# Left rows of the output projections on 128 rows, value products with a pair of heads as weights, and high weights of two branches by ScalarE in a float32 decoder trunk

## The chip, the cores and the metric

One core of one Trainium2 chip runs the whole program. The time is device microseconds of one execution; less is better. The engines are TensorE (PE, with its weight loads, PEld), VectorE (DVE), ScalarE (ACT), GpSimd (POOL) and SyncE (SP), which issues the weight transfers. Each engine works through its instructions in order; waits between engines are semaphores.

## What is computed

Two layers of a decoder trunk on 256 tokens of width 1024, all in float32. A layer is a gated feed-forward block, a mixer, a cross-attention to 256 memory tokens, and a second feed-forward block. The change lies in the mixer:

```python
proj = h @ w_in
o_fox = fox_attention(fq, fk, fv, log_f).reshape(b, s, FOX_W)                           # 6 heads of 64
o_dsa = dsa_sparse_attention(dq, dk, dv, q_idx, k_idx, w_idx, topk).reshape(b, s, DSA_W)  # 5 heads
o_sb = stick_breaking_attention(sq, sk, sv).reshape(b, s, SB_W)                          # 5 heads
g = jax.nn.sigmoid(gates.reshape(b, s, N_BRANCH, D_MODEL))
merged = g[:, :, 0] * (o_fox @ w_fox_out) + g[:, :, 1] * (o_dsa @ w_dsa_out) + g[:, :, 2] * (o_sb @ w_sb_out)
return merged @ w_out
```

So the output projections contract over 384, 320 and 320 rows: three chunks of 128 rows for the first branch, two chunks of 128 and 64 left rows for the other two. In all three an attention probability matrix P of 256x256 is multiplied with the head's values, out = P V, which is the value product.

## The kernel before

**Float32 by parts.** A matrix product runs on operands that are split in a high part (rounded to the fp32r format) and a low part (the rest): high x high, high x low and low x high are added up in one accumulator (`mm3`, lines 139 to 141). The activations are split once (`split`, lines 153 and 154: ACT writes the high part, DVE the low part). The weights come by SP into `wraw` (three buffers) and are split as they come, in `load_w`: the high part `wh` by ACT (`high`, line 92) or by DVE (line 90), as `share["high"]` says, and the low part `wl` by DVE or POOL (`sub_split`, line 86). `wh` and `wl` have five buffers each.

**The left rows.** Where a weight has 64 left rows (320 = 2 x 128 + 64), `load_w` makes one block of 128 rows out of them (lines 128 to 133): rows 0 to 63 of `wl` hold the high part (a copy by ACT, line 131), rows 64 to 127 the low part. The activation's high part stands twice, in rows 0 to 63 and in rows 64 to 127 (`osplit`, line 482). Then two products do for three (`mm2`): line 145 on 128 rows gives high x high and low x high together, line 146 on 64 rows gives high weight x low activation.

**The mixer.** `softmax_pv` takes one head's logits to probabilities, transposes them on PE (line 592) and calls `pv`: two matmuls with the head's 64 columns of values as weights and the probabilities as the moving operand (lines 599 and 600). The first head of a pair writes rows 0 to 63 of a PSUM bank `ops`, the second rows 64 to 127. There is one such bank. The stick-breaking branch computes the probabilities of two heads at once and calls `pv` for both, one behind the other. The last head of branches two and three stands alone in its bank. `osplit` then splits the bank in high and low, `osp`.

**The output projections** come after the heads (lines 771 to 787). All twelve gates pass the sigmoid in a row on ACT, between two loads of its function tables. Each branch has two weight loads of 512 columns, and each load two column blocks of 256, which take one of three accumulator banks `acc`. A block is six groups of products (two halves by three chunks). DVE multiplies the block with its gate (line 783), which frees the bank; POOL adds it to the branch before (line 785). While these weights are loaded, `share["high"]` is "DVE", so DVE casts all high parts (line 90) and ACT makes only the copies of left rows. Behind this stage comes the keys' projection of the cross-attention, then the mixer's last projection.

**The order** of each engine's instructions is set by a scheduler when the program is built; the code of these parts names no order. So the change also moves instructions that it does not touch.

Of the kernel before, what the change touches and what calls it, by code (L numbers as in the profile page):

```python
# [9 lines left out]
F32 = mybir.dt.float32  # L10
# [22 lines left out]
def trunk(ctx: ExitStack, tc: tile.TileContext, x, mem, positions, ffn1_norm, ffn1_w_gu, ffn1_w_down,  # L33
# [20 lines left out]
    def o_ps():  # L54
        return psum.tile([128, 512], F32, name="ops", bufs=1)
# [41 lines left out]
    def load_w(cols, first=None):  # L97
# [6 lines left out]
        for g in first or groups(-(-rows // 128), 2048 // n):  # L104
# [14 lines left out]
            for gg in groups(g, 1024 // n):  # L119
                h = wts.tile([128, 1024], F32R, name="wh", bufs=5)  # L120
                lo = lows.tile([128, 1024], F32R, name="wl", bufs=5)
                b = min(k1 + gg, full)
                if b > k1:
                    r, o = raw[:, k1 * n:b * n], slice(0, (b - k1) * n)
                    high(h[:, o], r)
                    sub_split(lo[:, o], r, h[:, o])
                    res += [(h[:, j * n:(j + 1) * n], lo[:, j * n:(j + 1) * n]) for j in range(b - k1)]
                if k1 + gg > full:
                    r, o = raw[:, full * n:(full + 1) * n], slice((full - k1) * n, (full - k1 + 1) * n)
                    high(h[:, o], r)  # L130
                    ACT.activation(lo[:64, o], r[:64], AF.Copy)
                    sub_split(lo[64:, o], r[64:], h[64:, o])
                    res.append((h[:64, o], lo[:, o]))
                k1 += gg
# [8 lines left out]
    def mm2(ps, a, b, first, last):  # L143

        PE.matmul(ps, a[1], b[0], start=first, stop=False)
        PE.matmul(ps, a[0], b[1], start=False, stop=last)  # L146

# [312 lines left out]
    def mixer_cross(l):  # L460
# [4 lines left out]
        with tc.tile_pool(name="mix", bufs=1) as mp:  # L465
# [10 lines left out]

            def osplit(ps, n):
                h = mp.tile([128, S], F32R, name="osp", bufs=18)
                lo = mp.tile([128, S], F32R, name="osp", bufs=18)
                split(h[:n], lo[:n], ps[:n])  # L480
                if n < 128:
                    ACT.activation(h[64:], ps[:64], AF.Copy)
                return (h, lo[:n])

# [92 lines left out]

            def softmax_pv(lg, v, h, ot, b):

# [14 lines left out]
                ACT.activation(pT, ps[:, :384], AF.Copy)  # L594
                pv(ot, b, v, h, pT[:, 0:256], pT[:, 256:384])

            def pv(ot, b, v, h, p0, p1):
                o = ot[b:b + 64, :]
                PE.matmul(o, v[0][:, h * 64:(h + 1) * 64], p0, start=True, stop=False)  # L599
                PE.matmul(o[:, 128:256], v[1][:, h * 64:(h + 1) * 64], p1, start=False, stop=True)  # L600

            def tok_v(pss, n):
                res = []
                for t in range(2):
                    v = mp.tile([128, 384], F32, name="vtok", bufs=4)
                    ACT.activation(v[:, :n], pss[t][:, :n], AF.Copy, scale=rc[t])
                    res.append(v)
                return res
# [37 lines left out]
            for j in range(NFOX // 2):  # L646
# [4 lines left out]
                for c, n in ((0, 128), (256, 256)):  # L651
                    for i, ps in enumerate(bank):
                        b = slice(64 * i, 64 * i + 64)
                        PE.matmul(ps[:, c:c + n], fqk[j][b, c // 2:c // 2 + 128], fqk[3 + j][b, 0:n],  # L654
                                  start=False, stop=c == 256)
                ot = o_ps()[:, :256]
                for i, ps in enumerate(bank):
# [5 lines left out]
                                             op0=OP.add, op1=OP.add)  # L663
                    softmax_pv(lg, fv, h, ot, 64 * i)
                ofox.append(osplit(ot, 128))

# [11 lines left out]
            for j in range(3):  # L678
                nh = 2 if j < 2 else 1
                bank = scores(dT[0][j], dT[1][j], nh)  # L680
                ot = o_ps()[:, :256]
                for i, ps in enumerate(bank):
                    lg = w384()
                    DVE.tensor_tensor(lg, ps[:, :384], dmask, op=OP.add)
                    softmax_pv(lg, dv, 2 * j + i, ot, 64 * i)
                odsa.append(osplit(ot, 64 * nh))

# [28 lines left out]
            for j in range(3):  # L716
# [30 lines left out]
                tact(az, zm, AF.Exp)  # L747
                ot = o_ps()[:, :256]
                for i in range(nh):
                    pv(ot, 64 * i, sv, 2 * j + i, az[:, i, 0:256], az[:, i, 256:384])  # L750
                osb.append(osplit(ot, 64 * nh))


# [17 lines left out]
            merged = []  # L771
            share["high"], share["pool"] = "DVE", 0
            for br, (wo, ot) in enumerate(((w_fox_out, ofox), (w_dsa_out, odsa), (w_sb_out, osb))):
                for cc in range(2):
                    w = load_w([wo[l][:, cc * 512:(cc + 1) * 512]])
                    for c in (2 * cc, 2 * cc + 1):
                        ps = acc_ps()
                        for s in range(2):
                            for k in range(3):
                                mm = mm2 if br and k == 2 else mm3  # L780
                                mm(ps[:, s * 256:(s + 1) * 256], cols(w[k], 2 * (c % 2) + s), ot[k], k == 0, k == 2)
                        g = gates[br * 4 + c]
# [92 lines left out]
            for kt in range(2):  # L875
                for h in range(NCA):
                    PE.matmul(ots[h], vm[kt][:, h * 128:(h + 1) * 128], pT[h][:, kt], start=kt == 0, stop=kt == 1)
            oc = [osplit(ot, 128) for ot in ots]
            for c in range(4):
# [43 lines left out]
```

## Time and profile before

| what | before |
|---|---|
| median of 3 runs | 1345.66 us (1345.48 to 1345.84) |
| the profiled execution | 1345.4 us, its span 1343.7 us |
| PE busy | 1328.5 us, 99% of the span, 10746 matmuls |
| DVE, ACT, POOL busy | 905.8 (67%), 719.0 (54%), 292.8 us (22%) |
| granted clock of PE, mean | 0.998 |
| the chain that ended last | PE 94%, DVE 3% |
| DMA | 234.65 MB, mean 175 GB/s |

The span is the time from the first to the last instruction in the trace. The busy time of PE is counted with modelled ends, and matmuls overlap, so the cost of a product is read from the distance of starts. The chain is the work followed back from the last instruction, at each step to what released it. A float32 matmul that is not split in parts (lines 592, 599, 600 and 877) shows as two passes in the timeline, so one value product of a head counts as two rows of each of its two lines.

### The profile page before, as it was taken

Reading aid. Unit: us, or ns where it says so; the run is one execution under the profiler, and the core shown is the slowest. Engines: PE = TensorE matmul, PEld = TensorE weight load, DVE = VectorE, ACT = ScalarE, POOL = GpSimd, SP = SyncE. Lnnn points to the kernel's source line nnn. Section 1 sums busy time; section 2 is a strip of 40 time slices with the busy share of each in tenths; the row PEclk is TensorE's granted clock in tenths of the full one; section 3 lists DMA queues with packets and bytes.
Section 4 is the critical chain, followed back from the end, with each engine's and each line's share of the span. In section 5 each row is a group of like instructions: output and inputs, shape, how many; then the busy total and the mean of one; then the engine's idle time right before and its main releaser. Section 6 shows DMA issues by size and latency. Waiting matters only on the chain.

```text
span 1343.7 us, 26241 instructions
## 1 busy us (share of the span) xinstructions
PE 1328.5 (99%) x10746; PEld 1275.6 (95%) x10746; DVE 905.8 (67%) x1397; ACT 719.0 (54%) x1149; POOL 292.8 (22%) x257
## 2 busy tenths in 40 slices
PE   8999999999999999999999999999999999999998
PEld 7999998989999999999999999999989899999987
DVE  7866556965689776665666665668567886766643
ACT  6555544545754565554465554444556556655543
POOL 3211114421313122111121110334223320311100
PEclk9999999999999999999999999999999999999999
DMA  7665654645446455566655566646453554566551
GB/s 252 192 198 192 208 167 146 186 118 160 133 127 210 153 177 174 190 197 202 198 188 189 188 205 193 186 124 207 118 158 119 165 190 165 166 198 200 198 183 67
DMA packets 220712, 234.65 MB, mean 175 GB/s; under 512 B 8656, under 2 KB 209968, under 8 KB 220592
## 3 DMA queue, kind: packets, MB, share of 16 engines
q1 hardware_dynamic: 219904, 231.87, 54.3%
q8 instruction: 84, 1.38, 0.4%
q0 software_dynamic: 240, 0.55, 0.1%
q10 hardware_dynamic: 448, 0.57, 0.1%
q14 instruction: 36, 0.29, 0.1%
HBM read 231.91 MB, written 1.05 MB: 173 GB/s over the span
## 4 chain that ended last, share of the span: by engine, by line
PE 94%; DVE 3%; DMA 1%; POOL 1%; issue 1%; ACT 0%; SPq 0%; DVEq 0%; ACTq 0%; POOLq 0%
PE acc L139 29%; PE acc L141 28%; PE acc L140 28%; PE ops L599 1%; PE qk L543 1%; DMA wraw<-in_ffn_w_gu_dram 1%; PE acc L146 1%; DVE wl L86 1%; PE tr L592 1%; PE qk L728 1%; PE qk L654 1%; PE ops L600 0%; DVE sc L573 0%; POOL it L517 0%; PE qk L825 0%
## 5 line engine op out<-in xcount | busy, mean ns | idle before, releaser
L86 DVE TENSOR_TENSOR wl<-wraw,wh 128x1024 fp32r<-128x1024 f32 (+6 forms) x429 | 510.9, 1194 | 225.4 <-ACT wh L92 218.5
L92 ACT ACTIVATE wh<-wraw 128x1024 fp32r<-128x1024 f32 (+4 forms) x447 | 446.0, 1003 | 274.1 <-PE acc L140 177.1
L141 PE MATMUL acc<-xh,wl 128*128 128x256 f32 x2032 | 564.5, 278 | 1.6 <-DVE wl L86 1.6
L140 PE MATMUL acc<-xl,wh 128*128 128x256 f32 x2032 | 564.4, 278 | 0.0
L139 PE MATMUL acc<-xh,wh 128*128 128x256 f32 x2032 | 563.9, 279 | 0.0
L141 PEld LDWEIGHTS acc<-xh,wl 128*128 128x128 f32 x2032 | 381.5, 188 | 4.4 <-DVE wl L86 2.2
L140 PEld LDWEIGHTS acc<-xl,wh 128*128 128x128 f32 x2032 | 381.8, 188 | 3.3 <-issue 3.0
L139 PEld LDWEIGHTS acc<-xh,wh 128*128 128x128 f32 x2032 | 380.9, 188 | 4.0 <-issue 3.5
L383 POOL TENSOR_TENSOR hm<-sg,gu 128x256 f32<-128x256 f32 x88 | 84.7, 963 | 385.6 <-ACT sg L69 385.6
L141 PE MATMUL acc<-hh,wl 128*128 128x256 f32 x528 | 145.4, 276 | 0.0
L140 PE MATMUL acc<-hl,wh 128*128 128x256 f32 x528 | 145.4, 276 | 0.0
L139 PE MATMUL acc<-hh,wh 128*128 128x256 f32 x528 | 144.4, 276 | 0.0
L86 POOL TENSOR_TENSOR wl<-wraw,wh 128x1024 fp32r<-128x1024 f32 (+3 forms) x42 | 88.1, 2099 | 220.0 <-ACT wh L92 198.9
L69 ACT ACTIVATE sg<-gu 128x256 f32<-128x256 f32 x88 | 36.7, 417 | 121.1 <-DVE gu L379 121.1
L140 PEld LDWEIGHTS acc<-hl,wh 128*128 128x128 f32 x528 | 99.1, 188 | 0.0
L141 PEld LDWEIGHTS acc<-hh,wl 128*128 128x128 f32 x528 | 99.1, 188 | 0.0
L139 PEld LDWEIGHTS acc<-hh,wh 128*128 128x128 f32 x528 | 98.5, 188 | 0.0
L379 DVE TENSOR_TENSOR gu<-acc,rs_r 128x512 f32<-128x512 f32 x88 | 60.3, 686 | 42.6 <-PE acc L141 42.5
L230 POOL TENSOR_TENSOR sqa<-sqa,sq 128x256 f32<-128x256 f32 x54 | 48.9, 905 | 146.3 <-ACT sq L225 144.9
L154 DVE TENSOR_TENSOR hl<-hm,hh 128x256 fp32r<-128x256 f32 x88 | 37.0, 421 | 42.5 <-ACT hh L153 42.3
L153 ACT ACTIVATE hh<-hm 128x256 fp32r<-128x256 f32 x88 | 36.1, 410 | 53.8 <-POOL hm L383 53.7
L141 PE MATMUL acc<-wh,xl 128*128 128x320 f32 (+1 forms) x192 | 61.3, 319 | 0.0
(282 smaller groups left out, 1988.2 us busy)
## 6 DMA issues: line engine op xcount, KB each, us to landing
wraw<-in_ffn_w_gu_dram SPq DMA_DIRECT2D x87, 1024.0 KB, 5.2
wraw<-in_w_in_dram SPq DMA_DIRECT2D x34, 1024.0 KB, 5.5
wraw<-in_ffn_w_down_dram SPq DMA_DIRECT2D x28, 896.0 KB, 5.0
wraw<-in_ffn_w_down_dram SPq DMA_DIRECT2D x18, 1024.0 KB, 5.2
wraw<-in_w_in_dram SPq DMA_DIRECT2D x20, 640.0 KB, 4.1
wraw<-in_ca_w_kv_dram SPq DMA_DIRECT2D x8, 1024.0 KB, 5.0
wraw<-in_w_out_dram SPq DMA_DIRECT2D x8, 1024.0 KB, 5.0
wraw<-in_ca_w_q_dram SPq DMA_DIRECT2D x4, 1024.0 KB, 5.3
```

The source lines that it names most:

```text
L69: i = ACT.activation(*a, **k)
L86: share["last"] = eng.tensor_tensor(lo, raw, h.bitcast(F32), op=OP.subtract)
L92: ACT.activation(h, raw, AF.Copy)
L139: PE.matmul(ps, a[0], b[0], start=first, stop=False)
L140: PE.matmul(ps, a[0], b[1], start=False, stop=False)
L141: PE.matmul(ps, a[1], b[0], start=False, stop=last)
L146: PE.matmul(ps, a[0], b[1], start=False, stop=last)
L153: ACT.activation(h, src, AF.Copy)
L154: DVE.tensor_tensor(lo, src, h.bitcast(F32), op=OP.subtract)
L230: POOL.tensor_tensor(n, sqacc[0], sq, op=OP.add)
L379: DVE.tensor_tensor(gu, ps.rearrange("p (i n) -> p i n", i=2), rb2(r), op=OP.mult)
L383: POOL.tensor_tensor(hm, sg, gu[:, 1], op=OP.mult)
```

## The change

Three edits, and what the scheduler makes of them.

1. `load_w` writes the high part of left rows only in rows 64 to 127 of `wh` (from which the low part is formed), and gives back one block of weights, `lo`. `mm2` multiplies this same block of 128 rows twice, with the activation's high block (line 145 of the changed kernel) and with its low block (line 146), whose rows 64 to 127 are zero for a head that stands alone.
2. `pv` takes the 128 columns of a pair of heads as weights and writes all 128 rows of one half of the bank; head h uses half h % 2. The rows of the other head in that half are not read. `tok_v` sets the columns behind 320 to zero on POOL. `hsplit` takes the place of `osplit` for heads: it splits each head's 64 rows by themselves, so four steps for a pair instead of two; for a head alone it adds the copy of the high part (ACT) and a copy of zeros (DVE) into rows 64 to 127.
3. `share["high"]` is "DVE" for the first branch's output weights as before, and "ACT" for the second and third.

```diff
@@ -127,10 +127,10 @@
                     res += [(h[:, j * n:(j + 1) * n], lo[:, j * n:(j + 1) * n]) for j in range(b - k1)]
                 if k1 + gg > full:
                     r, o = raw[:, full * n:(full + 1) * n], slice((full - k1) * n, (full - k1 + 1) * n)
-                    high(h[:, o], r)
                     ACT.activation(lo[:64, o], r[:64], AF.Copy)
+                    high(h[64:, o], r[64:])
                     sub_split(lo[64:, o], r[64:], h[64:, o])
-                    res.append((h[:64, o], lo[:, o]))
+                    res.append((lo[:, o],))
                 k1 += gg
             k0 += g
         return res
@@ -142,8 +142,8 @@
 
     def mm2(ps, a, b, first, last):
 
-        PE.matmul(ps, a[1], b[0], start=first, stop=False)
-        PE.matmul(ps, a[0], b[1], start=False, stop=last)
+        PE.matmul(ps, a, b[0], start=first, stop=False)
+        PE.matmul(ps, a, b[1], start=False, stop=last)
 
     def cols(w, s):
         return [v[:, s * 128:(s + 1) * 128] for v in w]
@@ -474,13 +474,23 @@
             def w384():
                 return mp.tile([128, 384], F32, name="w384", bufs=5)
 
-            def osplit(ps, n):
+            def osplit(ps):
                 h = mp.tile([128, S], F32R, name="osp", bufs=18)
                 lo = mp.tile([128, S], F32R, name="osp", bufs=18)
-                split(h[:n], lo[:n], ps[:n])
-                if n < 128:
-                    ACT.activation(h[64:], ps[:64], AF.Copy)
-                return (h, lo[:n])
+                split(h, lo, ps)
+                return (h, lo)
+
+            def hsplit(ot, nh):
+
+                h = mp.tile([128, S], F32R, name="osp", bufs=18)
+                lo = mp.tile([128, S], F32R, name="osp", bufs=18)
+                for i in range(nh):
+                    b = slice(64 * i, 64 * i + 64)
+                    split(h[b], lo[b], ot[b, i * 256:(i + 1) * 256])
+                if nh == 1:
+                    ACT.activation(h[64:], ot[:64, :256], AF.Copy)
+                    DVE.tensor_copy(lo[64:], cneg[64:].bitcast(F32))
+                return (h, lo)
 
             def proj_tok(c0, n, bank=acc_ps):
 
@@ -575,7 +585,7 @@
             POOL.tensor_tensor(dmask, dmask, cmask, op=OP.add)
 
 
-            def softmax_pv(lg, v, h, ot, b):
+            def softmax_pv(lg, v, h, ot):
 
                 nm = mp.tile([128, 2], F32, name="nm", bufs=4)
                 sm = mp.tile([128, 2], F32, name="sm", bufs=4)
@@ -592,18 +602,22 @@
                     PE.transpose(ps[:, j * 128:(j + 1) * 128], p[:, j * 128:(j + 1) * 128], ident)
                 pT = w384()
                 ACT.activation(pT, ps[:, :384], AF.Copy)
-                pv(ot, b, v, h, pT[:, 0:256], pT[:, 256:384])
-
-            def pv(ot, b, v, h, p0, p1):
-                o = ot[b:b + 64, :]
-                PE.matmul(o, v[0][:, h * 64:(h + 1) * 64], p0, start=True, stop=False)
-                PE.matmul(o[:, 128:256], v[1][:, h * 64:(h + 1) * 64], p1, start=False, stop=True)
+                pv(ot, v, h, pT[:, 0:256], pT[:, 256:384])
+
+            def pv(ot, v, h, p0, p1):
+
+                o = ot[:, h % 2 * 256:(h % 2 + 1) * 256]
+                c = slice(h // 2 * 128, h // 2 * 128 + 128)
+                PE.matmul(o, v[0][:, c], p0, start=True, stop=False)
+                PE.matmul(o[:, 128:256], v[1][:, c], p1, start=False, stop=True)
 
             def tok_v(pss, n):
                 res = []
                 for t in range(2):
                     v = mp.tile([128, 384], F32, name="vtok", bufs=4)
                     ACT.activation(v[:, :n], pss[t][:, :n], AF.Copy, scale=rc[t])
+                    if n < 384:
+                        POOL.memset(v[:, n:], 0.0)
                     res.append(v)
                 return res
 
@@ -653,7 +667,7 @@
                         b = slice(64 * i, 64 * i + 64)
                         PE.matmul(ps[:, c:c + n], fqk[j][b, c // 2:c // 2 + 128], fqk[3 + j][b, 0:n],
                                   start=False, stop=c == 256)
-                ot = o_ps()[:, :256]
+                ot = o_ps()
                 for i, ps in enumerate(bank):
                     h = 2 * j + i
                     lg = w384()
@@ -661,8 +675,8 @@
                                              op0=OP.add, op1=OP.add)
                     DVE.scalar_tensor_tensor(lg[:, 128:384], ps[:, 256:512], cq[:, 1, h:h + 1], cmask[:, 128:384],
                                              op0=OP.add, op1=OP.add)
-                    softmax_pv(lg, fv, h, ot, 64 * i)
-                ofox.append(osplit(ot, 128))
+                    softmax_pv(lg, fv, h, ot)
+                ofox.append(hsplit(ot, 2))
 
 
             dT = []
@@ -678,12 +692,12 @@
             for j in range(3):
                 nh = 2 if j < 2 else 1
                 bank = scores(dT[0][j], dT[1][j], nh)
-                ot = o_ps()[:, :256]
+                ot = o_ps()
                 for i, ps in enumerate(bank):
                     lg = w384()
                     DVE.tensor_tensor(lg, ps[:, :384], dmask, op=OP.add)
-                    softmax_pv(lg, dv, 2 * j + i, ot, 64 * i)
-                odsa.append(osplit(ot, 64 * nh))
+                    softmax_pv(lg, dv, 2 * j + i, ot)
+                odsa.append(hsplit(ot, nh))
 
             gates = []
 
@@ -745,10 +759,10 @@
                 DVE.tensor_tensor(zm[:, :, 0:256], p0, zm[:, :, 0:256], op=OP.add)
                 DVE.tensor_tensor(zm[:, :, 256:384], p1[:, :, 0:128], zm[:, :, 256:384], op=OP.add)
                 tact(az, zm, AF.Exp)
-                ot = o_ps()[:, :256]
+                ot = o_ps()
                 for i in range(nh):
-                    pv(ot, 64 * i, sv, 2 * j + i, az[:, i, 0:256], az[:, i, 256:384])
-                osb.append(osplit(ot, 64 * nh))
+                    pv(ot, sv, 2 * j + i, az[:, i, 0:256], az[:, i, 256:384])
+                osb.append(hsplit(ot, nh))
 
 
             mgn = []
@@ -769,16 +783,20 @@
 
 
             merged = []
-            share["high"], share["pool"] = "DVE", 0
+            share["pool"] = 0
             for br, (wo, ot) in enumerate(((w_fox_out, ofox), (w_dsa_out, odsa), (w_sb_out, osb))):
+                share["high"] = "ACT" if br else "DVE"
                 for cc in range(2):
                     w = load_w([wo[l][:, cc * 512:(cc + 1) * 512]])
                     for c in (2 * cc, 2 * cc + 1):
                         ps = acc_ps()
                         for s in range(2):
                             for k in range(3):
-                                mm = mm2 if br and k == 2 else mm3
-                                mm(ps[:, s * 256:(s + 1) * 256], cols(w[k], 2 * (c % 2) + s), ot[k], k == 0, k == 2)
+                                a, o = cols(w[k], 2 * (c % 2) + s), ps[:, s * 256:(s + 1) * 256]
+                                if br and k == 2:
+                                    mm2(o, a[0], ot[k], False, True)
+                                else:
+                                    mm3(o, a, ot[k], k == 0, k == 2)
                         g = gates[br * 4 + c]
                         DVE.tensor_tensor(g, ps.rearrange("p (i n) -> p i n", i=2), g, op=OP.mult)
                         if br:
@@ -875,7 +893,7 @@
             for kt in range(2):
                 for h in range(NCA):
                     PE.matmul(ots[h], vm[kt][:, h * 128:(h + 1) * 128], pT[h][:, kt], start=kt == 0, stop=kt == 1)
-            oc = [osplit(ot, 128) for ot in ots]
+            oc = [osplit(ot) for ot in ots]
             for c in range(4):
                 w = load_w([ca_w_o[l][:, c * 256:(c + 1) * 256]])
                 for s in range(2):
```

PE's count of matmuls is the same, and so is SP's list of transfers. DVE has 16 casts of weights less, 14 low parts of heads more and 4 copies of zeros; ACT has 16 high parts of weights and 14 high parts of heads more; POOL has 8 memsets more.

How the order moves, at three places. The names: `t2` are gates, `osp` the split outputs of heads, `acc` the accumulator banks, `wraw`, `wh` and `wl` a weight load as it came, its high and its low part; the number behind a name tells buffers apart.

ACT in layer 1, from the last two sigmoids on, before:

```order
L69 ACTIVATE t2_4794<-t2_4794 128x512
L69 ACTIVATE t2_4855<-t2_4855 128x512
L64 ACT_TABLE_LOAD
L153 ACTIVATE osp_4321<-ops_4318 64x256
L131 ACTIVATE wl_4980<-wraw_4971 64x512
L131 ACTIVATE wl_5031<-wraw_5022 64x512
L482 ACTIVATE osp_4321<-ops_4318 64x256
L131 ACTIVATE wl_5082<-wraw_5073 64x512
L131 ACTIVATE wl_5133<-wraw_5124 64x512
```

and with the change:

```order
L69 ACTIVATE t2_4814<-t2_4814 128x512
L69 ACTIVATE t2_4875<-t2_4875 128x512
L64 ACT_TABLE_LOAD
L153 ACTIVATE osp_4340<-ops_4337 64x256
L92 ACTIVATE wh_4999<-wraw_4991 64x512
L130 ACTIVATE wl_5000<-wraw_4991 64x512
L92 ACTIVATE wh_5046<-wraw_5042 128x1024
L92 ACTIVATE wh_5050<-wraw_5042 64x512
L92 ACTIVATE wh_5097<-wraw_5093 128x1024
L491 ACTIVATE osp_4340<-ops_4337 64x256
L92 ACTIVATE wh_5101<-wraw_5093 64x512
```

Behind the sigmoids and the table load, ACT had only the copies of left rows to make; now the high parts of left rows and of whole blocks stand among them (line 92), the first ahead of the first copy of left rows (line 130). One high part of 1024 columns of the second branch stands ahead of the exponential that precedes the sigmoids.

DVE in layer 1, from the second gate multiply of the first branch on (line 783 before, 801 now), before:

```order
L783 TENSOR_TENSOR t2_3796<-acc_4901,t2_3796 128x512
L86 TENSOR_TENSOR wl_4980<-wraw_4971,wh_4979 64x512
L86 TENSOR_TENSOR wl_5027<-wraw_5022,wh_5026 128x1024
L783 TENSOR_TENSOR t2_3857<-acc_4931,t2_3857 128x512
L90 CAST wh_5030<-wraw_5022 128x512
L154 TENSOR_TENSOR osp_4322<-ops_4318,osp_4321 64x256
L90 CAST wh_5077<-wraw_5073 128x1024
L783 TENSOR_TENSOR t2_3918<-acc_4951,t2_3918 128x512
L86 TENSOR_TENSOR wl_5031<-wraw_5022,wh_5030 64x512
L86 TENSOR_TENSOR wl_5078<-wraw_5073,wh_5077 128x1024
L783 TENSOR_TENSOR t2_3979<-acc_4984,t2_3979 128x512
L90 CAST wh_5081<-wraw_5073 128x512
```

and with the change:

```order
L801 TENSOR_TENSOR t2_3809<-acc_4921,t2_3809 128x512
L801 TENSOR_TENSOR t2_3870<-acc_4951,t2_3870 128x512
L801 TENSOR_TENSOR t2_3931<-acc_4971,t2_3931 128x512
L154 TENSOR_TENSOR osp_4341<-ops_4337,osp_4340 64x256
L86 TENSOR_TENSOR wl_5000<-wraw_4991,wh_4999 64x512
L86 TENSOR_TENSOR wl_5047<-wraw_5042,wh_5046 128x1024
L86 TENSOR_TENSOR wl_5051<-wraw_5042,wh_5050 64x512
L801 TENSOR_TENSOR t2_3992<-acc_5004,t2_3992 128x512
L86 TENSOR_TENSOR wl_5098<-wraw_5093,wh_5097 128x1024
L801 TENSOR_TENSOR t2_4509<-acc_5023,t2_4509 128x512
L86 TENSOR_TENSOR wl_5102<-wraw_5093,wh_5101 64x512
L86 TENSOR_TENSOR wl_5149<-wraw_5144,wh_5148 128x1024
```

The gate multiplies of the first branch now follow on each other, and the low parts of the second branch (line 86), which alternated with them, come behind them and behind the low part of the last head's output (line 154).

PE in layer 2, at the matrix products that the last exponential of stick-breaking waits for (`spl` and `sph` are its operands), before:

```order
L740 MATMUL qk_12408<-spl_12397,negu_75 128x256
L742 MATMUL qk_12408<-sph_12396,negones_76 128x128
L742 MATMUL qk_12408<-spl_12397,negones_76 128x128
L744 MATMUL qk_12409<-spl_12397,negu_75 128x128
L141 MATMUL acc_12907<-xh6_88,wl_12904 128x256
L139 MATMUL acc_12907<-xh7_89,wh_12903 128x256
L140 MATMUL acc_12907<-xl7_97,wh_12903 128x256
L141 MATMUL acc_12907<-xh7_89,wl_12904 128x256
L139 MATMUL acc_12982<-osp_11264,wh_12974 128x256
```

and with the change:

```order
L141 MATMUL acc_13022<-osp_11343,wl_13015 128x256
L139 MATMUL acc_13022<-osp_11402,wh_13018 128x256
L754 MATMUL qk_12447<-spl_12436,negu_75 128x256
L756 MATMUL qk_12447<-sph_12435,negones_76 128x128
L756 MATMUL qk_12447<-spl_12436,negones_76 128x128
L758 MATMUL qk_12448<-spl_12436,negu_75 128x128
L140 MATMUL acc_13022<-osp_11403,wh_13018 128x256
L141 MATMUL acc_13022<-osp_11402,wl_13019 128x256
L139 MATMUL acc_13042<-osp_11284,wh_13014 128x256
```

The last `spl` products stood 8 to 5 rows ahead of the first product of the first branch's output projection (the last row of the first piece). Now they stand 18 to 21 rows behind it. In layer 1 they stood 24 to 21 rows ahead of it, and now 5 to 2.

## Rows read from the trace of the kernel before

**Rows 1.** The page: PE's clock in 40 slices; the chain that ended last.

```profile
PEclk9999999999999999999999999999999999999999
...
PE 94%; DVE 3%; DMA 1%; POOL 1%; issue 1%; ACT 0%; SPq 0%; DVEq 0%; ACTq 0%; POOLq 0%
```

**Rows 2.** Timeline of PE, first products of the output projections in both layers.

```profile
388.55 0.28 PE L139 MATMUL acc<-osp,wh 128*128 128x256 f32 x1
...
389.12 0.28 PE L141 MATMUL acc<-osp,wl 128*128 128x256 f32 x1
...
1047.08 0.28 PE L139 MATMUL acc<-osp,wh 128*128 128x256 f32 x1
...
1058.52 0.28 PE L145 MATMUL acc<-osp,wl 128*128 128x256 f32 x1
```

**Rows 3.** Timeline of PE, a half-row product (start us, us, engine, line, operation, out<-in).

```profile
399.11 0.28 PE L145 MATMUL acc<-osp,wl 128*128 128x256 f32 x1
399.32 0.38 PE L146 MATMUL acc<-osp,wh 64*128 64x256 f32 x1
399.63 0.39 PE L139 MATMUL acc<-osp,wh 128*128 128x256 f32 x1
399.85 0.28 PE L140 MATMUL acc<-osp,wh 128*128 128x256 f32 x1
399.97 0.28 PE L141 MATMUL acc<-osp,wl 128*128 128x256 f32 x1
```

**Rows 4.** Timeline of PE, the value product of one head alone.

```profile
268.89 0.28 PE L650 MATMUL qk<-cneg,sel 128*128 128x256 f32 x1
269.10 0.64 PE L599 MATMUL ops<-w,vtok 128*64 128x256 f32 x2
...
269.90 0.39 PE L650 MATMUL qk<-cneg,sel 128*128 128x256 f32 x1
```

**Rows 5.** Timeline of ACT, layer 1, around the sigmoids (idle before, releaser).

```profile
387.27 0.53 ACT L69 ACTIVATE az<-zm 128x384 f32<-128x384 f32 x1 [1.34 <-DVE zm L746]
...
389.11 6.36 ACT L69 ACTIVATE t<-t 128x512 f32<-128x512 f32 x12
...
397.06 1.18 ACT L131 ACTIVATE wl<-wraw 64x512 fp32r<-64x512 f32 x2
```

**Rows 6.** Timeline of ACT, layer 2, the first copies of left rows.

```profile
1057.11 1.14 ACT L131 ACTIVATE wl<-wraw 64x512 fp32r<-64x512 f32 x2
```

**Rows 7.** Busy time by windows: PE, PEld, DVE, ACT, POOL, clock, DMA.

```profile
397.00:416.00 19.00, 19.00 (x121) 15.51 (x119) 18.38 (x22) 6.36 (x10) 8.75 (x6) 1.00 0.69 207
```

**Rows 8.** DVE's subtractions: mean from 397 to 420 us, then single ones.

```profile
L86 DVE TENSOR_TENSOR wl<-wraw,wh 128x1024 fp32r<-128x1024 f32 x6 | 10.1, 1691 | 0.1
...
404.93 1.66 DVE L86 TENSOR_TENSOR wl<-wraw,wh 64x512 fp32r<-64x512 f32 x1
...
407.23 1.21 DVE L86 TENSOR_TENSOR wl<-wraw,wh 128x1024 fp32r<-128x1024 f32 x1
...
1069.61 0.69 DVE L86 TENSOR_TENSOR wl<-wraw,wh 64x512 fp32r<-64x512 f32 x1
```

**Rows 9.** Timeline of PE, the cross-attention's value products on the full array.

```profile
479.57 0.39 PE L141 MATMUL acc<-wh,t 128*128 128x512 f32 x1
479.80 0.59 PE L877 MATMUL ops<-t,mi 128*128 128x256 f32 x2
480.23 1.03 PE L877 MATMUL tr<-t,mi 128*128 128x256 f32 x4
```

**Rows 10.** Timeline of PE, the value products of two stick-breaking heads.

```profile
360.76 0.66 PE L599 MATMUL ops<-az,vtok 128*64 128x256 f32 x4
...
361.57 0.39 PE L141 MATMUL acc<-xh,wl 128*128 128x256 f32 x1
```

**Rows 11.** Timeline of PE and DVE: a pair's last value product and its split.

```profile
292.95 0.38 PE L600 MATMUL ops<-w,vtok 128*64 128x128 f32 x2
...
294.65 0.42 DVE L154 TENSOR_TENSOR osp<-ops,osp 128x256 fp32r<-128x256 f32 x1
```

## The prediction, made before the changed kernel was run

> **What bounds the kernel now.** I read the page first: TensorE (PE) takes 94% of the chain that ended last, and its clock row stands at 9 or more in every slice [rows 1], so work taken off PE is time unless it uncovers a wait. The timeline of PE then gives the price of each form. In the output projections two full products start 0.114 us apart (six starts from 388.55 to 389.12) [rows 2]. Around a half-row product the starts at 399.11, 399.32, 399.63, 399.85 and 399.97 are 0.21, 0.31, 0.22 and 0.12 apart [rows 3]. A value product of one head takes from 269.10 to 269.90, 0.80 us, and the work before it stands 0.21 [rows 4]. Last come the other engines in the stage of the output projections, since PE's weights come from there [rows 5 to 8].
>
> I count time from P, the first fox product of that stage: 388.55 in layer 1, and P2 = 1047.08 in layer 2 [rows 2].
>
> **Left rows on 128 rows.** The count of PE instructions stays. Four steps from 399.11 to 399.97 take 0.86 where four full ones would take 0.46, so a pair with a half-row product costs 0.40 extra. There are 32 pairs (2 layers, 2 branches, 4 column blocks, 2 halves): 32 x 0.40 = **12.9 us off PE**. Bounds: 12.9, and 0 only if the time is not that of the tile's shape; the slow steps stand on both sides of the 64-row product and nowhere else, so I take 12.9. The sum's other new work here (16 casts fewer on DVE, 16 more high parts on ACT) is priced below, where it waits.
>
> **Value products on 128 columns.** Of 32 heads 24 run alone and 8 in pairs (the two pairs of stick-breaking heads in each layer). A lone head costs 1.01 from 268.89 to 269.90; take off the 0.114 that the product at 268.89 costs anyway, and add 0.11, by which the next step after a change of shape is long (399.63 to 399.85 against 399.85 to 399.97): 1.01. The trace of before has no such product on 128 columns. The nearest is the cross-attention's value product on the full array: a pass of 256 rows takes 0.215 (479.80 to 480.23 for two), and it starts 0.23 after a wide product, which is that product's own time, so entry costs nothing [rows 9]. A head is two such passes and two of half the length, 2 x 0.215 + 2 x 0.108 = 0.65. Saved: 0.36 if entry and exit fall away, 0.15 if only the body (0.80) shrinks. I take 0.35, close to the upper end, since the nearest row shows the entry without a price [rows 9]: 24 x 0.35 = **8.4 off**; the lower end is 3.6. For a pair of stick-breaking heads the trace shows the contrary: two heads in halves of the columns take 360.76 to 361.57, 0.81, no more than one [rows 10]. With 128 columns each they run one after the other, 1.30, less the 0.22 of entry and exit: 0.27 more, times 4 pairs = **1.1 added**.
>
> The Trainium skill, "TensorEngine Tiling (Array Packing)", Overview, speaks against this edit: a left side of 64 columns or fewer may gain up to 2x from column tiles. The trace agrees for the pairs [rows 10] and not for the lone heads [rows 4]; if lone halves were as quick as the rule says, the 8.4 would be nothing and the sum 1342.4 (that case is inside the forecast's far bound).
>
> **Off PE in all: 12.9 + 8.4 - 1.1 = 20.2 us.**
>
> **Splits by head.** Each pair's output is split in four steps instead of two, 64 rows each; a zero copy and a copy of the high part come in for single heads. They lie beside PE's products. Their price is how long the one output bank is held, which is 2.1 us after the last value product before (292.95 to 294.65 + 0.42) [rows 11]. The shortest distance from one pair's last value product to the next pair's first is 44 PE rows in the new order, 44 x 0.114 = 5.0 us. Nothing at 4.2 (doubled); it costs beyond 5 (a rival below). POOL's eight memsets of 64 columns stand before the heads begin and have no reader close by: nothing. If those covers went, a pair's split would cost its overhang. No DMA moves on SP's queue.
>
> **High weights by ACT.** This is where a wait comes. ACT works in order, and behind the last exponential of stick-breaking stand a table load, twelve sigmoids (6.36 us) and another table load [rows 5]. Before, the high parts of the second and third branch were cast on DVE meanwhile. Now one 128x1024 high part stands ahead of the exponential; its cover is ACT's idle 1.34 there [rows 5]. The rest stand behind the sigmoids: first a 64x512 high part, then the 64x512 copy of the left rows. The first half-row pair of the second branch waits for both. The exponential moves too: the matrix products that feed it end 19 rows later against P in layer 1 and 26 in layer 2, so by 19 x 0.113 = 2.15 and 26 x 0.113 = 2.94 us.
>
> Layer 1: ACT's copy of left rows started at 397.06, P + 8.51; two of its size take 1.18 [rows 5]. So the data is there at P + 8.51 + 2.15 + 1.18 = P + 11.84. PE came to that product at 399.11, P + 10.56 [rows 2, 3], with the same 86 rows ahead now, of which one head is 0.35 quicker: P + 10.21. **Wait 1.6 us.** Layer 2: 1057.11 is P2 + 10.03 [rows 6]; + 2.94 + 1.14 = P2 + 14.1. PE came at 1058.52, P2 + 11.44 [rows 2]; 92 rows as before, four of them now half as long (-0.23), one head quicker (-0.35): P2 + 10.86. **Wait 3.25 us.** Together **4.9 back**.
>
> **DVE behind it.** DVE also works in order: its low parts wait for ACT's high parts, and behind them stand the gate multiplies that free PE's three accumulator banks. In the stage before, DVE was busy 18.4 of 19 us [rows 7]. Beside POOL's adds its subtractions ran long: six of 1691 ns in the mean against 1.21 alone, and one of 64x512 of 1.66 against 0.69 [rows 8], 6 x 0.48 + 0.97 = 3.9 us. The casts that go relieve DVE; but it starts the rest later, and can no longer work ahead. So PE meets between 0 (all that surplus in DVE's gaps) and 3.9 us in each layer. I take the middle, 1.95: the 0.6 us of gaps [rows 7] speaks for the upper end, the five casts that leave this stretch for the lower. **3.9 back** for both.
>
> The Trainium skill, "SBUF — State Buffer", Who interferes with whom, says that a VectorE instruction with two inputs in SBUF and a GpSimd instruction that reads SBUF shut each other out for their whole length. The long subtractions agree in kind; if every add blocked DVE for its whole length, the second rival would be the likelier.
>
> **Sum.** 20.2 - 4.9 - 3.9 = 11.4 us. The profiled execution took 1345.4 (span 1343.7), 0.26 under the median of the three runs, 1345.66: 1345.4 - 11.4 = **1334.0 us**. Its own bounds: 1330.1 with DVE's term at nothing, 1337.9 with it at 3.9 each, 1342.7 with the lone heads at 0.15 as well.
>
> **Rivals.**
> 1. *No wait stands.* If the sigmoid chain is earlier than I have it (the order tells places, not times), all 20.2 us come out: 1325.2. For it: ACT is idle half the time. Against: ACT's queue is in order, and the first copy of left rows ended only about 1.4 us ahead of PE before [rows 3, 5]. Chance 0.14.
> 2. *DVE becomes the bound.* Each of POOL's 8 adds per layer lengthens a DVE instruction by about 0.8 (0.48 in the mean, 0.97 in the longest) [rows 8], 6.5 us per layer, and DVE has no gap: 20.2 - 4.9 - 13.0 = 2.3, 1343.1, no change. For it: the 18.4 of 19. Against: the casts are gone. Chance 0.10.
> 3. *Slower: the output bank.* The split's four hand-overs alternate between ACT and DVE, each behind whatever stands queued there (a subtraction is 1.21 alone) [rows 8]. If each costs some 2 us, the bank is held 8 us; it decides from 5.0 us on. Seven distances of the new order lie under 62 rows (44, 47, 47, 51, 55, 56, 61: 5.0 to 7.0 us), and overhang together 8 x 7 - 361 x 0.114 = 14.8 us. 1334.0 + 14.8 = 1348.8. For it: one bank. Against: with two hand-overs it was 2.1 [rows 11]. Chance 0.06.
> 4. *The change doesn't do what it says:* the slow steps [rows 3] belong to the left-row products themselves, whatever their rows. 12.9 stays away: 1346.9, no change. Against: the full product that follows is slow too. Chance 0.02.
>
> **How the numbers follow.** Forecast 0.68, rival 1 0.14, rival 2 0.10, rival 3 0.06, rival 4 0.02. About 0.2%, 2.7 us, is what a measurement here tells from no change: faster is under 1343.0, slower over 1348.3. Faster: 0.68, less 0.02 for what lies beyond its far bound, 0.14, and 0.03 of rival 2, which straddles the line: 0.83. Same: 0.02 + 0.07 + 0.02 = 0.11. Slower: 0.06. The range takes in rival 1, the forecast's bounds and the near edge of rival 2, 1325.0 to 1342.7; left out are rivals 3 and 4, most of rival 2 and the forecast's odd remainder, 0.17.
>
> **What would show it.** Right: the two products of the left rows on 128 rows at steps of 0.114; a lone head in 0.65; a PE wait of 1 to 4 us at the second branch's first left-row product in each layer, released by ACT's copy; ACT without a gap from the sigmoids to the high parts; shorter waits for DVE's gate multiplies after it. Wrong: steps of 0.2 and 0.3 that remain; lone heads at 0.8; no wait there; PE waiting for the output bank between heads, in the attention stage.

## The result, and the profile after

The changed kernel takes 1338.61 us (median of 4, 1337.81 to 1339.76) against 1345.57: a ratio of 0.9949, interval 0.9932 to 0.9966. That is 7.0 us less; forecast were 11.4, and the range 1325.0 to 1342.7 holds it. The profiled execution is the slowest of the four, 1339.76, so the trace below shows 5.6 us and not 7.0.

| | before | after |
|---|---|---|
| span | 1343.7 us | 1338.0 us |
| PE busy | 1328.5 us | 1313.6 us |
| PE's share of the chain that ended last | 94% | 89% |
| start of the stage to the keys' projection, layer 1 | 30.34 us | 28.35 us |
| the same, layer 2 | 30.49 us | 31.62 us |

The stage is the one that the prediction speaks of, from the first fox product to line 139's first product with `t` (418.89 and 1077.57 before, 414.19 and 1072.02 after). PE has 14.9 us of busy time less, and the span only 5.7: the rest became idle time. The waits of PE in the new trace (engine, line, waited for, us in all, times, longest):

```profile
PE acc L145 <- DVE wl L86: 5.9, 2, 4.2
...
PE acc L139 <- DVE t L801: 2.1, 3, 1.4
...
PE acc L145 <- ACT wl L130: 1.0, 1, 1.0
```

None of the three stood before. The steps of PE around left-row products in layer 1, the answer to [rows 3], and a lone head, the answer to [rows 4]:

```profile
398.88 0.28 PE L145 MATMUL acc<-osp,wl 128*128 128x256 f32 x1
398.99 0.28 PE L146 MATMUL acc<-osp,wl 128*128 128x256 f32 x1
399.10 0.28 PE L145 MATMUL acc<-osp,wl 128*128 128x256 f32 x1
399.22 0.28 PE L146 MATMUL acc<-osp,wl 128*128 128x256 f32 x1
...
268.88 0.28 PE L664 MATMUL qk<-cneg,sel 128*128 128x256 f32 x1
269.00 0.59 PE L611 MATMUL ops<-w,vtok 128*128 128x256 f32 x2
...
269.57 0.36 PE L664 MATMUL qk<-cneg,sel 128*128 128x256 f32 x1
```

Apart from the first wait and two steps of 0.19, every left-row product of layer 1 now starts 0.11 after the product before it. The lone head takes 0.57 from 269.00 to 269.57, and entry 0.12. Behind the logits' products on 64 rows it is different:

```profile
320.35 0.92 PE L553 MATMUL qk<-t,t 64*128 64x128 f32 x4
321.20 0.70 PE L611 MATMUL ops<-w,vtok 128*128 128x256 f32 x2
...
321.88 0.36 PE L140 MATMUL acc<-xl,wh 128*128 128x256 f32 x1
```

There the head takes 0.68, and the step into it 0.31. Now layer 2, PE and then ACT and DVE, which answer to [rows 2] and [rows 6]:

```profile
1055.80 0.40 PE L145 MATMUL acc<-osp,wl 128*128 128x256 f32 x1 [4.23 <-DVE wl L86]
1056.02 0.39 PE L146 MATMUL acc<-osp,wl 128*128 128x256 f32 x1
...
1059.20 0.40 PE L140 MATMUL acc<-osp,wh 128*128 128x256 f32 x1
1059.41 0.30 PE L141 MATMUL acc<-osp,wl 128*128 128x256 f32 x1
1059.55 0.28 PE L145 MATMUL acc<-osp,wl 128*128 128x256 f32 x1
```
```profile
1044.23 0.53 ACT L69 ACTIVATE az<-zm 128x384 f32<-128x384 f32 x1 [1.72 <-DVE zm L760]
...
1046.07 6.36 ACT L69 ACTIVATE t<-t 128x512 f32<-128x512 f32 x12
...
1053.74 0.63 ACT L130 ACTIVATE wl<-wraw 64x512 fp32r<-64x512 f32 x1
1054.39 1.71 ACT L92 ACTIVATE wh<-wraw 64x512 fp32r<-64x512 f32 x2
...
1055.05 0.69 DVE L86 TENSOR_TENSOR wl<-wraw,wh 64x512 fp32r<-64x512 f32 x1 [4.05 <-ACT wh L92]
```

PE stands 4.23 us until DVE has the low part of the left rows, DVE stands 4.05 until ACT has the high part, and ACT has just come out of the sigmoids. Then PE runs at half speed: the 17 steps from 1055.80 to 1059.41 take 0.21 each instead of 0.11, 1.7 us in all. The windows of PE (us, PE busy, granted clock, DMA) show why:

```profile
1048.00:1052.00 4.00, 3.57 (x32) 1.00 0.01 2
1052.00:1056.00 4.00, 0.20 (x1) 1.00 0.01 2
1056.00:1060.00 4.00, 4.00 (x22) 0.57 0.62 197
1060.00:1064.00 4.00, 4.00 (x37) 1.00 0.86 272
```

After the long wait the clock was granted at half, 1.2 instead of 2.4 GHz, for some 3.4 us (a mean of 0.57 over 4 us). The Trainium skill, "TensorE: Matmul & The Clock Gate", Part 1, says that an idle array is throttled to half its clock and activity releases it; this trace agrees.

### The profile page after: what moved, and what is told of

It is laid out like the page before. It is cut to its first block, busy times and chain, and to the rows that moved or that the text cites. A ratio compares the mean times of both kernels' runs of the same rounds, so it can differ in the third digit from the quotient of the medians.

```text
span 1338.0 us, 26300 instructions
## 1 busy us (share of the span) xinstructions
PE 1313.6 (98%) x10746; PEld 1277.9 (96%) x10746; DVE 902.2 (67%) x1399; ACT 738.7 (55%) x1179; POOL 297.2 (22%) x265
## 4 chain that ended last, share of the span: by engine, by line
PE 89%; DVE 4%; ACT 3%; issue 1%; DMA 1%; POOL 1%; DVEq 0%; ACTq 0%; POOLq 0%
PE acc L139 27%; PE acc L141 27%; PE acc L140 27%; DVE wl L86 2%; PE qk L553 1%; PE ops L611 1%; ACT t L69 1%; POOL it L527 1%; DMA wraw<-in_ffn_w_gu_dram 1%; ACT wh L92 1%; PE tr L602 1%; PE qk L668 1%; PE qk L742 1%; PE ops L612 0%; DVE sc L583 0%
## 5 line engine op out<-in xcount | busy, mean ns | idle before, releaser
L92 ACT ACTIVATE wh<-wraw 128x1024 fp32r<-128x1024 f32 (+5 forms) x463 | 459.2, 997 | 259.1 <-PE acc L140 156.0
```

The costliest lines, as they stand in the source:

```text
L92: ACT.activation(h, raw, AF.Copy)
```

## The experiments

All runs are on the chip, against the kernel before on the same chip (1345.6 to 1345.8). The last two columns give the stage's length, P to the keys' projection, from the traces.

| run | median us | ratio, interval | layer 1 | layer 2 |
|---|---|---|---|---|
| before | 1345.6 | | 30.34 | 30.49 |
| the change | 1338.61 | 0.9949 [0.9932, 0.9966] | 28.35 | 31.62 |
| rows_only | 1337.91 | 0.9943 [0.9929, 0.9958] | 26.36 | 26.44 |
| heads_only | 1349.57 | 1.0037 [1.0013, 1.0062] | 30.27 | 36.71 |
| highs_only | 1348.99 | 1.0026 [1.0015, 1.0036] | 31.22 | 31.90 |
| highs_dve (rows and heads) | 1338.03 | 0.9944 [0.9927, 0.9960] | 27.23 | 31.18 |
| rows_highs | 1339.31 | 0.9953 [0.9939, 0.9968] | 26.69 | 27.71 |
| rows_sig | 1336.77 | 0.9935 [0.9918, 0.9951] | 25.31 | 25.76 |
| rows_highs_sig | 1331.86 | 0.9897 [0.9882, 0.9912] | 23.67 | 23.68 |
| sig_behind (all three) | 1330.05 | 0.9884 [0.9868, 0.9901] | 23.35 | 26.44 |
| after_spl | 1338.56 | 0.9949 [0.9935, 0.9964] | 28.34 | 28.78 |
| sig_spl | 1328.95 | 0.9875 [0.9859, 0.9892] | 23.35 | 24.24 |
| sig_spl_pairs | 1327.21 | 0.9862 [0.9847, 0.9876] | 23.39 | 24.15 |
| no_adds | 1336.17 | 0.9931 [0.9916, 0.9945] | 25.97 | 31.03 |

**One part alone.** `rows_only` has the change's left rows and `mm2`, and in the old `osplit`:

```diff
                 if n < 128:
                     ACT.activation(h[64:], ps[:64], AF.Copy)
-                return (h, lo[:n])
+                    DVE.tensor_copy(lo[64:], cneg[64:].bitcast(F32))
+                return (h, lo)
```

> The kernel before with the left rows on 128 rows alone; heads and DVE's casts as before. Theory M (the rows are worth 12.5 us on PE, but DVE, which was busy 18.4 of 19 us in the output projections, then sets the pace there): two to three of the 6.2 us per layer come out, time 1339 to 1342, the products themselves at steps of 0.114 and PE waiting for DVE's gate multiplies or low parts, 3 to 4 us per layer. Rival R (DVE works ahead enough): all comes out, 1333, no new PE waits.

Measured 1337.91, 0.7 under the change with all its parts. PE waits for the gate multiplies, and DVE is busy 24.59 of the stage's 26.36 us:

```profile
PE acc L139 <- DVE t L787: 3.4, 4, 1.4
...
387.95:414.31 26.36, 24.50 (x207) 23.45 (x205) 24.59 (x33) 15.03 (x24) 9.00 (x5) 1.00 0.62 180
```

That is theory M's mechanism, and half its waits: 7.8 us came out, more than the 4 to 6 it allowed, and the time is 1.1 below its range. `heads_only` has `pv`, `tok_v` and `hsplit` of the change, without the zeros, and the old left rows.

> The changed value products and splits by head alone; left rows on 64 rows and DVE's casts as before. Theory M: lone heads save 0.33 each, pairs cost 0.3 each, and neighbours on 64 rows keep the price of a change of shape: 3 to 5 us off PE, less a wait of 1 to 2 us in layer 2 because the last exponential comes later: 1341 to 1343. Rival R (the change of order upstream costs more than the products save): 1345 or more.

M missed: 1349.57. R has the time, not the reason, as the stretch upstream shows below. The ten executions spread from 1343.5 to 1358.6, their mean granted clock from 0.998 to 0.987. The profile (1346.8, among the quicker ones; the slow ones left no trace) shows the clock fall in layer 2, after waits of 1.1 and 1.2 us and while the left rows still run on 64 rows:

```profile
1056.00:1060.00 4.00, 3.14 (x15) 0.95 0.54 157
1060.00:1064.00 4.00, 4.00 (x15) 0.50 0.84 221
1064.00:1068.00 4.00, 4.00 (x20) 0.70 0.75 247
```

In the heads' stretch ahead of the stage the products gained as they should (first fox product at 385.54 instead of 388.55); the stage of layer 2 grew by 6.2 and took it back: 2.4 us of waits, and about 3.4 by the clock (0.05, 0.50 and 0.30 of 4 us each are missing in these windows). `highs_only` sets the high weights alone:

```diff
-            share["high"], share["pool"] = "DVE", 0
+            share["pool"] = 0
             for br, (wo, ot) in enumerate(...):
+                share["high"] = "ACT" if br else "DVE"
```

> The kernel before with the high weights of the second and third branch by ACT alone. Theory M (ACT's queue of sigmoids delays the weights): a PE wait of 1 to 2 us at the first left-row product of each layer, time 1347 to 1349. Rival R (the wait in the changed kernel came from the heads' later exponential, not from the place of the high parts): no wait, 1345.6.

1348.99, as M says, though the wait of 1.3 us stands in layer 2 alone, and what ended it is ACT's split of the last head, which stands in ACT's queue behind a high part and the copy:

```profile
PE acc L145 <- ACT osp L153: 1.3, 1, 1.3
```

With nothing else changed, ACT's high weights cost 3.3 us. The trace shows about 2 of them, since it is the quickest of eight executions (1347.47, mean clock 0.999); the slowest took 1350.65 at 0.996 and left no trace. `highs_dve` undoes this part in the change.

> The changed kernel with all high weights of the output projections cast by DVE as before. Theory M: the wait for ACT's high parts goes (4 to 6 us of the 6.9 at the first left-row products), but DVE's casts come back and it paces the stage: within 2 us of the changed kernel, 1337 to 1341. Rival R1 (the high parts by ACT are the whole loss): 1331 to 1333. Rival R2 (ACT's relief of DVE is what brings the gain): 1342 or more.

1338.03: 0.6 from the change, inside the spread of both. PE's wait at the first left-row product went, and waits for DVE's gate multiplies took its place:

```profile
PE acc L139 <- DVE t L800: 7.9, 7, 1.5
```

**The sigmoids.** `rows_highs` is `rows_only` with `highs_only`.

> Left rows on 128 rows and high weights by ACT, with the value products and splits of the kernel before, sigmoids where the changed kernel has them. Theory M (the late exponential that the heads' edit brings is about 2 to 3 us of each wait; without it the weights come 0 to 1.5 us late): waits at the first left-row products of 0 to 1.5 us per layer, 1335 to 1338, no slowed clock. Rival R (the ACT queue alone makes the waits): 3 to 4 us in layer 2 as in the changed kernel, 1339 or more.

1339.31, in R's range by the time and M's by the wait: the first left-row product of layer 2 waits 1.3 us, that of layer 1 not at all, and the clock stays; but 3.2 us of waits for gate multiplies follow, which M had left out.

```profile
PE acc L139 <- DVE t L788: 3.2, 2, 1.7
...
PE acc L145 <- DVE wl L86: 1.3, 1, 1.3
```

So of the change's 4.2 more than half came with the heads. The next edit leaves every instruction and holds eight sigmoids back:

```diff
-            for g in gates:
+            for g in gates[:4]:
                 tact(g, g, AF.Sigmoid)
-            table(LNEXP)
...
                     w = load_w([wo[l][:, cc * 512:(cc + 1) * 512]])
+                    if br:
+                        with tc.issue_after(share["copy"].ins):
+                            for g in gates[br * 4 + 2 * cc:br * 4 + 2 * cc + 2]:
+                                tact(g, g, AF.Sigmoid)
...
+            table(LNEXP)
             for c in range(4):
                 merged.append(t2(F32R))
```

where `share["copy"]` is the load's copy of left rows. In the change this is `sig_behind`:

> The changed kernel, with the sigmoids of the second and third branch held back behind the ACT pieces of their branch's weight loads, two gates behind each load; the second table load follows the last of them. Theory M (the 5.9 us at the first left-row products stand because ACT's high parts and copies queue behind eight sigmoids that nothing needs yet, and the slowed clock after the wait in layer 2 adds some 1.5 to 2 us): no wait over 0.5 us there, clock 1.00 throughout layer 2's stage, 1330 to 1333. Rival R (DVE's queue is the bound and takes the waits over): first waits gone, waits for DVE's gate multiplies grown by as much, 1336 to 1339.

1330.05, 8.6 us under the change. What is left of the waits in its stages:

```profile
PE acc L139 <- DVE t L804: 0.9, 1, 0.9
...
PE acc L145 <- ACT wl L130: 0.6, 1, 0.6
```

The 5.9 at the first left-row products are gone; the 0.6 stands at a later one of layer 2. DVE did not take them over, and the clock stays at 1.00, as the windows of PE in layer 2's stage show:

```profile
1044.00:1048.00 4.00, 4.00 (x38) 1.00 0.53 165
1048.00:1052.00 4.00, 3.44 (x31) 1.00 0.34 98
1052.00:1056.00 4.00, 4.00 (x36) 1.00 0.78 264
1056.00:1060.00 4.00, 3.05 (x27) 1.00 0.96 306
```

With the old heads it is `rows_highs_sig`:

> The same with the value products and splits of the kernel before: left rows on 128 rows, high weights by ACT, sigmoids held back. Theory M (the heads' edit is worth 3 to 5 us on PE once no wait hides it): 3 to 5 us slower than the run with it, 1333 to 1337. Rival R (the heads' edit is worth nothing, since it moves the last exponential and the changes of shape elsewhere): the same within 1 us, or quicker.

1331.86: the heads' edit is worth 1.8 us here, between the two theories. This trace has a stage without a single wait; window of layer 2, [rows 7] with all engines:

```profile
1040.49:1064.17 23.68, 23.68 (x207) 23.23 (x206) 20.19 (x26) 23.09 (x34) 10.54 (x6) 1.00 0.64 202
```

DVE is at 85%, and ACT, not DVE, is now nearly full. `rows_sig`, the same without ACT's high weights, tells whether they are needed:

> Left rows on 128 rows alone, DVE casting the high weights as before, with the sigmoids of the second and third branch held back behind their loads. Theory M (without ACT's help DVE sets the pace of the stage, so holding the sigmoids back brings nothing by itself): PE still waits 4 to 6 us in all for DVE's gate multiplies, 1336.5 to 1338.5. Rival R (the held-back sigmoids are the gain, and ACT's high weights are not needed for it): waits under 1 us, 1331.5 to 1333.

1336.77, M: 1.1 from the sigmoids alone, 4.9 more with the high weights on ACT. Waits for gate multiplies are 2.0 us instead of M's 4 to 6; the rest of its longer stage is PE's restarts after them and idle times too short for the list.

**The late exponential.** `after_spl` puts one wait into the change, ahead of the first fox product:

```diff
+                                elif br == cc == c == s == k == 0:
+                                    with tc.issue_after(share["spl"].ins):
+                                        mm3(o, a, ot[k], True, False)
```

> The changed kernel, with the first product of the output projections issued behind the last matrix product of stick-breaking; in layer 2 those products then stand 4 to 1 rows ahead of it instead of 18 to 21 behind, in layer 1 nothing moves. Theory M (of the 4.2 us wait in layer 2, about 2.5 come from the late exponential, and the slowed clock of 1.7 us follows from the length of that wait): the first left-row product of layer 2 waits 1.5 to 2 us as in layer 1, clock 1.00 there, 1333.5 to 1335.5. Rival R (the sigmoids' queue alone sets the wait, wherever the exponential stands): wait still 3.5 us or more, 1337 to 1339.

1338.56, a miss for M's sum; R has the time, but not the wait. The wait fell from 4.23 to 2.36, not to 1.5 to 2, and the clock fell all the same:

```profile
1054.43 0.36 PE L145 MATMUL acc<-osp,wl 128*128 128x256 f32 x1 [2.36 <-DVE wl L86]
...
1052.00:1056.00 4.00, 1.64 (x13) 0.95 0.13 19
1056.00:1060.00 4.00, 4.00 (x25) 0.62 0.60 194
```

The stage of layer 2 is 2.8 us shorter, but starts 1.6 us later against layer 1's end, since PE now makes the matrix products ahead of it and waits 0.5 us for their operands. The 1.2 us that are left lie within the spread of either kernel's executions (2.0 us). `sig_spl` has both edits, `sig_spl_pairs` also the pairs of stick-breaking heads back on 64 columns, with `osplit` for their bank.

> The run with sigmoids held back (1330.05), and in it the first product of the output projections behind the last matrix product of stick-breaking. Theory M (the 2.0 us of waits left in layer 2's stage come from the late exponential of that layer): both waits under 0.3 us, 1327 to 1328.5. Rival R (PE waits for the matrix products' operands instead): a new wait ahead of the stage, 1329.5 or more.

> The same, with the stick-breaking heads that run in pairs back on 64 columns each, so that they run side by side, and split as one. Theory M (a pair on 128 columns costs 0.3 us more than side by side, four pairs): 1.2 us less than the run before, 1326 to 1327.5. Rival R (the order moves by more than that): the same or slower by up to 1 us.

1328.95, between the theories: the stage of layer 2 gained 2.2 us, and 1.4 went to that wait ahead of it and to the products moved. 1327.21: 1.7 us for four pairs, 0.4 each. This is the quickest version, 11.4 us under the change.

**POOL's additions.** `no_adds` leaves out line 803.

> The changed kernel without POOL's sixteen additions of gated branches (the first two branches' products then do not reach the merged sum). Theory M (the additions lengthen DVE's subtractions, and that is the 3.1 us of later waits in the two stages): those waits under 1 us in all, first waits as they are, 1335 to 1336.5. Rival R (DVE's own queue is long enough without them): later waits stay, 1338 to 1339.5.

1336.17, M. DVE's subtractions of 1024 columns from 397 to 414 us, first with and then without the additions:

```profile
L86 DVE TENSOR_TENSOR wl<-wraw,wh 128x1024 fp32r<-128x1024 f32 x5 | 9.1, 1844 | 0.9 <-ACT wh L92 0.9
```
```profile
L86 DVE TENSOR_TENSOR wl<-wraw,wh 128x1024 fp32r<-128x1024 f32 x6 | 7.2, 1222 | 1.6 <-ACT wh L92 1.6
```

1844 against 1222 ns, and waits for gate multiplies fell from 2.1 to 0.2:

```profile
PE acc L139 <- DVE t L801: 0.2, 1, 0.2
```

The Trainium skill, "SBUF — State Buffer", Who interferes with whom, says that a VectorE instruction with two inputs in SBUF contends with a GpSimd instruction that reads SBUF; these two runs agree in kind. That the two shut each other out for their whole length, as the prediction puts it, no run shows: a subtraction grew by 0.62 us in the mean, and three additions took 5.30 (from 407.06 on). The additions cost the change 2.4 us. Most of it shows in layer 1's stage, 2.4 us shorter without them; layer 2's is only 0.6 shorter, because after the same wait of 4.23 us PE ran longer at half clock, 5.1 us (1053.59 to 1058.66) instead of 3.6:

```profile
1052.00:1056.00 4.00, 2.41 (x11) 0.50 0.30 87
1056.00:1060.00 4.00, 4.00 (x26) 0.67 0.72 226
```

## Why the prediction was right, and where it was off

- *Left rows, 12.9 off PE:* right. Without waits the two stages lose 6.67 and 6.81 us (`rows_highs_sig`).
- *Value products, 8.4 - 1.1 = 7.3:* **this term was mis-sized**. A lone head saves 0.33, near the price, where full products stand on both sides. Its parts were not as priced: the step into the head became normal, but the slow step behind it stayed (0.21, before 0.22), and the body came to 0.57 instead of 0.65, so that two misses met is luck. Eight of the 22 lone heads outside the two stages stand beside products of 64 rows or of 128 columns and take 0.65 to 0.74 instead of 0.57; the mean saving, steps in and out included, is 0.28, and the four pairs cost 1.2. Measured ahead of the stages: 2.71 in layer 1, and 1.99 from layer 1's keys to P2, 4.7 where the terms give 6.6, and 0.45 more for the stick-breaking products that moved behind P2. With the sigmoids held back the edit is worth 1.8 us (`sig_behind`, in which layer 2's stage still waits 1.5 us), 2.9 without the late exponential (`sig_spl`).
- *Waits at the first left-row products, 1.6 and 3.25:* the place and the queue were right. In layer 2 it was 4.23, over the 1 to 4 that was to show the forecast right: PE came at P2 + 11.0 as worked out (10.86) and the data at P2 + 15.40 instead of 14.1. The exponential stood at P2 + 3.83; before it stood at P2 + 0.23 (the line below), and with the 2.94 that gives 3.17. And behind the copy of left rows came the high part, then DVE's subtraction, which ended last. I had counted two ACT pieces and no subtraction. The releaser was DVE, not ACT's copy. In layer 1 the wait was 1.66, but that fits in part by luck: there the high part came ahead of the copy, so the subtraction ran beside the copy (the other two lines) and added only 0.07.

```profile
1047.31 0.53 ACT L69 ACTIVATE az<-zm 128x384 f32<-128x384 f32 x1 [3.09 <-DVE zm L746]
```
```profile
397.02 0.63 ACT L130 ACTIVATE wl<-wraw 64x512 fp32r<-64x512 f32 x1
...
397.03 0.69 DVE L86 TENSOR_TENSOR wl<-wraw,wh 64x512 fp32r<-64x512 f32 x1 [0.23 <-ACT wh L92]
```

- *DVE behind it, 3.9:* 3.1 us of waits, at the gate multiplies (2.1) and at a later copy of left rows (1.0). Right in size; `no_adds` shows POOL's part in it.
- *The clock:* missing from the sum, 1.7 us in layer 2. I took it as given because its row stood at 9 or more in every slice before.
- *The output bank (rival 3):* no wait for it in any run.

Forecast and result differ by 4.6 us; in the profiled execution, by 5.8: some 2.4 from the heads, 1.0 from layer 2's wait and 1.7 from the clock. The 0.7 left is a balance: PE's restarts after its six waits cost some 2 us, an estimate from the steps (layer 1's first wait is 1.66 us of idle time, but 1.83 from start to start beyond a normal step), while left rows gave 0.6 more than forecast and DVE's waits were 0.8 smaller. The mechanism held: work came off PE, and waits, the largest of them behind the sigmoids, gave back more than half.

## What to carry to other kernels

Work taken off the bounding engine moves the bound to whatever fed it with little slack: 13.5 us came off this stage only once ACT made the weights and nothing that could wait stood ahead of them in its queue. Look at what stands in an in-order queue between the last urgent piece and the next one, and hold the rest back by an explicit dependency, since a scheduler need not see it. And price a value product or any small matmul with the neighbours it will have, not alone.

## What was not expected of the hardware

A wait of PE can cost more than its length. After 4.23 us without a product the clock was granted at half, and PE's steps were slow for 3.6 us; in `no_adds` they were slow for 5.1 us after a wait of the same length. It fell after 2.36 us in `after_spl` as well; after the 1.66 us in layer 1 it did not. In `heads_only` it fell after two shorter waits, and there the time of one kernel spread over 15 us; `highs_only` spread over 3. Both have the left rows on 64 rows; `rows_only` and `highs_dve`, on 128 rows, met waits of 1.4 to 1.5 us in layer 2, and their executions stayed within 1 us of each other. What sets it in these cases was not tried.
